# A PEER encoder layer on one core: packed rows, their waits, pinned TensorE work and smaller caps

## The chip, the core and the metric

The kernel runs on one core of a Trainium2 chip. The time is device time in microseconds (us) of one execution; several executions are timed and their median is given, and one more execution is recorded by the profiler. Engines by their names in the profile: PE is TensorE (PEld its weight loads), DVE is VectorE, ACT is ScalarE, POOL is GpSimd, SP is SyncE, which here only issues DMAs. Each engine, and each issuing queue, runs its instructions in order.

## The reference

One encoder layer for 256 tokens of width 2048: a mixer (grouped attention and a bidirectional mLSTM), cross-attention, and a PEER layer, each followed by a layer norm. The change touches the PEER layer only. There each token has 8 heads, and each head picks 16 of 16384 single-neuron experts by product keys; `u` and `v` hold one row of 2048 for each expert:

```python
experts = jnp.take_along_axis(cand_e..., best_pos, axis=-1)     # 128 experts per token
gates = jax.nn.softmax(best_s, axis=-1)
def block(args):
    xb, eb, gb = args
    a = jax.nn.gelu(jnp.einsum('ted,td->te', u[eb], xb), approximate=False) * gb
    return jnp.einsum('te,ted->td', a, v[eb])
```

## The kernel before

The PEER part computes the hidden values of *all* experts for all tokens, multiplies them by gates that are zero for what a token did not pick, and then brings only the experts that some token picked into a packed table, in whose order the rows of `v` are fetched.

U phase: the experts go in 32 quads of 512. `Ugen(q)` (L745) projects the 256 tokens on quad q in four chunks; each loads 1 MB of `u` into one of 5 `raw` buffers (`u_r`, L140, on SP), splits it in a high part (ScalarE, L103) and a low part (VectorE, L104), and runs 24 matmuls (L156, L157, L160). After the fourth chunk ScalarE applies Gelu (`gh`, L752). 11 quads (`LEAD`) run ahead while experts and gates are worked out; the gates go to DRAM (`gate_dram`, L812).

A phase: `Agen(q)` transposes `gh` of quad q on TensorE (L946, tile `ta`), multiplies by the gates (`G`, one load of 1 MB per two quads, L900; L949), writes the dense rows to DRAM (L959) and issues four indirect scatters on POOL (L962), each of 128 expert rows into `table`. Where a row goes is worked out for each pair g of quads in two steps: `route(g)` loads `G` and marks with masks M which expert serves both token tiles, only the first or only the second (kinds 0, 1, 2); `places(g, M)` counts them with two small matmuls (L914, L915; tile `pp`), scans, and leaves indices in `idx`. The table has room for `CAPS` tiles of 128 rows of each kind. An `Agen` gives way at three points: after each half of the transposes and after the scatters; that of quad 0 at seven more, between `route(0)` and `places(0)`.

V phase: `Vstage(n, lo, hi)` works on the table's tiles between two entries of `STAGES`, in two halves of 1024 columns. An entry such as `(16, (4, 2, 2))` says: once 16 scatters are out, 4, 2 and 2 tiles of the kinds are full. For one or two tiles it loads packed rows (`ar`, L1013, on SP), splits them (`ah`, `al`), gathers rows of `v` on POOL (L1024), splits these (`vh`, `vl`) and adds with three matmuls for each token tile and column block into PSUM (`o`, L1036): 24 matmuls for both halves of a tile of kind 0, 12 for one of kinds 1 and 2. From quad 14 (`VFROM`) on, U's sums lie in other PSUM banks and the `o` tiles have those of before.

The order in which these are traced is written out at the end: behind each chunk of U come `a_step` (three steps of `Agen` per chunk until the buffers of the first quads are given to `v`, then two) and `v_step` (some 3.6 us of V work per chunk, from quad 14 on; a stage starts 3 steps after its scatters were traced). The framework then places every instruction on its engine's queue by a simulated timeline, so it may run ahead of its traced order where its inputs are thought to be there sooner. After the loop a flag says whether the caps were overrun; if so, a branch does the V part densely.

The waits of the table loads are made by hand:

```python
for x in scat[covered[0]:]:
    tc.add_manual_dep(ins.ins, x.name, sync_data, reason="rows of the table")
covered[0] = len(scat)
```

`scat` holds all scatters traced so far, and each load waits for those that no load before it has waited for.

Of the kernel before, what the change touches and what calls it, by code (L numbers as in the profile page):

```python
# [18 lines left out]
P = 128  # L19
T = 256  # L20
# [9 lines left out]
LEAD = 11  # L30
# [5 lines left out]

CAPS = (53, 32, 32)
BASE = (0, CAPS[0], CAPS[0] + CAPS[1])  # L40
PLACES = sum(CAPS) * P
STAGES = ((16, (4, 2, 2)), (40, (13, 7, 7)), (72, (25, 14, 14)), (96, (34, 19, 19)), (112, (40, 23, 23)), (128, CAPS))


def body(tc, x, xT, memT, w_inA, w_inB, b_igate, b_fgate, att_q_norm, att_k_norm, ml_norm, w_out,
# [4 lines left out]
    V, S, G, PE = nc.vector, nc.scalar, nc.gpsimd, nc.tensor  # L50
# [37 lines left out]
    ident = cp.tile([P, P], F32, name="ident")  # L88
# [570 lines left out]
    table = dram.tile([PLACES, ROW], F32, name="table")  # L659
# [86 lines left out]
    ghs = {}  # L746
# [143 lines left out]
    nv = [0]  # L890
    Gt = {}
    run = [run0]
    scat = []
    covered = [0]
    sync_data = mybir.DependencyInfo(mybir.DependencyClass.Sync, mybir.DependencyReason.DATA)
# [14 lines left out]

    def places(g, M):
        pp = tp_tile(f"pp{g}")
        Mf = M.rearrange("p k i -> p (k i)")
        PE.matmul(pp[:, 0:24], before_m, Mf, start=True, stop=True)  # L914
        PE.matmul(pp[:, 24:48], ones_m, Mf, start=True, stop=True)  # L915
        inc = rtp.tile([P, 3, 8], F32, name=f"inc{g}", tag="inc")
        for k in range(3):
            V.tensor_tensor_scan(inc[:, k], pp[:, 24 + 8 * k:32 + 8 * k], zero8, run[0][:, k:k + 1], ALU.add, ALU.add)
        end = rtp.tile([P, 3], F32, name=f"end{g}", tag="end")
        V.tensor_copy(end, inc[:, :, 7])  # L920
        run[0] = end
        for n, (rows, _) in enumerate(STAGES):
            if rows == 8 * g + 8:
                V.tensor_copy(chk[:, n], inc[:, :, 7])
        V.tensor_tensor(inc.rearrange("p k i -> p (k i)"), inc.rearrange("p k i -> p (k i)"), pp[:, 24:48], ALU.subtract)
        V.tensor_tensor(inc.rearrange("p k i -> p (k i)"), inc.rearrange("p k i -> p (k i)"), pp[:, 0:24], ALU.add)
        V.tensor_tensor(inc, inc, M, ALU.mult)
        pf = rtp.tile([P, 8], F32, name=f"pf{g}", tag="pf")
        V.tensor_reduce(pf, inc.rearrange("p k i -> p i k"), AX.X, ALU.add)
        V.tensor_scalar(idx[:, g * 8:g * 8 + 8], pf, FAR, None, ALU.add)  # L930


    def Agen(q):
        if q == 0:
            M = route(0)
# [6 lines left out]
        for b in range(2):  # L942
            tp = tp_tile(f"ta{q}_{b}")
            for a in range(2):
                for t in range(NT):
                    PE.transpose(tp[:, a * T + t * P:a * T + (t + 1) * P],  # L946
                                 ghs[q][:, t, (2 * b + a) * P:(2 * b + a + 1) * P], ident)
            for a in range(2):
                V.tensor_tensor(r[:, 2 * b + a, :T].rearrange("p (c t) -> p c t", c=16),  # L949
                                tp[:, a * T:(a + 1) * T].rearrange("p (c t) -> p c t", c=16),  # L950
                                gg[:, :, (q % 2) * 4 + 2 * b + a, :], ALU.mult)
            if q % 2 == 1 and q + 1 < nq:
                if b == 0:
                    M = route((q + 1) // 2)
                else:
                    places((q + 1) // 2, M)
            yield
        ghs.pop(q)
        nc.sync.dma_start(dense[q], r)  # L959
# [29 lines left out]
    def Vstage(n, lo, hi):  # L989
# [9 lines left out]
        for half in range(2):  # L999
# [9 lines left out]
            for _, k, s0, w in order:  # L1009
# [1 line left out]
                ar = arp.tile([P, 2, ROW], F32, name=f"ar{nm}", tag="ar")[:, :w]  # L1011
                r0 = (BASE[k] + s0) * P
                ins = nc.sync.dma_start(ar, table[r0:r0 + w * P, :].rearrange("(p g) w -> p g w", p=P))  # L1013
                for x in scat[covered[0]:]:
                    tc.add_manual_dep(ins.ins, x.name, sync_data, reason="rows of the table")
                covered[0] = len(scat)
                tc.add_to_no_dep_group("table", ins.ins)
                c0, cw = ((0, T), (0, P), (P, P))[k]
                ah = ahp.tile([P, 2, T], F32R, name=f"ah{nm}", tag="ah")
# [211 lines left out]
```

## Time and profile before

| what | value |
|---|---|
| timed executions, median (3) | 2230.35 us (2224.93 to 2233.83) |
| profiled execution, whole | 2223.21 us |
| its span, first to last instruction | 2221.1 us |
| TensorE busy | 2120.2 us (95%) |
| VectorE, ScalarE, POOL busy | 1494.2, 1107.4, 452.7 us |
| matmuls of o (L1036) | 3 groups of 680 |
| scatters, gathers of v, table loads | 128, 234, 128 |

Times inside the execution are counted from the span's start. An engine's busy time counts its own instructions, not its waits; where an instruction waited, the profile names the idle time before it and the event that came last. The granted clock is a share of TensorE's full 2.4 GHz; it has two levels, 1.0 and 0.5, so a mean between them says for which part of a stretch the lower one held. The DMA share is the mean busy share of the core's 16 DMA engines.

### The profile page before, as it was taken

The page shows a single profiled execution, that of the slowest core. Times are in us where ns is not written, and L with a number is a line of the kernel's source. Part 1 is how long each engine was busy: PE and PEld are TensorE (multiplying, and loading weights), DVE is VectorE, ACT ScalarE, POOL GpSimd, SP SyncE. Part 2 cuts the span into 40 slices and gives each one's busy share as a digit, 9 for nine tenths or more (in the row PEclk, how much of TensorE's full clock was granted, in tenths as well). Part 3 has the DMA queues.
Part 4 walks back from the last instruction along what each step waited for, and adds up shares of the span by engine and source line. Part 5 has one row for each costly group of instructions (what it writes and reads, how often), then busy time and mean ns, then how long its engine had stood idle before and what let it go on. Part 6 is the DMA issues. An engine that isn't in the chain of part 4 may idle for free.

```text
span 2221.1 us, 28155 instructions
## 1 busy us (share of the span) xinstructions
PE 2120.2 (95%) x9794; PEld 1742.2 (78%) x9794; DVE 1494.2 (67%) x2678; ACT 1107.4 (50%) x1577; POOL 452.7 (20%) x402
## 2 busy tenths in 40 slices
PE   8899989999999899999997889999999999989996
PEld 6788868888888788888886668888877887868874
DVE  5765657664445679999785676676656656647776
ACT  4544635434443444579883244545454444536663
POOL 0000000000000000000002563443143434237661
PEclk9999989999999999999998989999999999989998
DMA  7543586565434345556668995987686778659994
GB/s 249 186 152 134 174 242 227 173 225 190 171 133 165 139 171 204 192 195 225 209 216 287 325 376 200 352 293 275 219 318 242 289 266 293 234 186 359 339 324 148
DMA packets 149479, 516.12 MB, mean 232 GB/s; under 512 B 14160, under 2 KB 59148, under 8 KB 113360
## 3 DMA queue, kind: packets, MB, share of 16 engines
q1 hardware_dynamic: 107504, 375.04, 48.7%
q0 software_dynamic: 39840, 137.19, 16.9%
q10 hardware_dynamic: 1984, 2.01, 0.3%
q8 instruction: 79, 1.29, 0.2%
q14 instruction: 72, 0.59, 0.1%
HBM read 457.72 MB, written 58.88 MB: 233 GB/s over the span
## 4 chain that ended last, share of the span: by engine, by line
PE 63%; issue 7%; DMA 5%; DVE 2%; POOL 2%; ACT 0%; POOLq 0%; DVEq 0%; SPq 0%; ACTq 0%
PE o L1036 17%; PE u_ps L156 8%; PE u_ps L160 8%; PE u_ps L157 8%; PE gp L808 3%; DMA table<-row,idx 2%; PE pq_ps L156 1%; PE wq_ps L160 1%; PE pq_ps L160 1%; PE pq_ps L157 1%; PE wq_ps L156 1%; PE wq_ps L157 1%; PE wv_ps L157 1%; PE wx_ps L156 1%; PE wx_ps L157 1%
## 5 line engine op out<-in xcount | busy, mean ns | idle before, releaser
L156 PE MATMUL u_ps<-u_h,x2T_h 128*128 128x512 f32 x1024 | 407.3, 398 | 4.3 <-ACT gh L752 4.3
L103 ACT CAST u_h<-u_r 128x1024 fp32r<-128x1024 f32 x256 | 268.7, 1051 | 275.0 <-PE u_ps L157 201.9
L157 PE MATMUL u_ps<-u_h,x2T_l 128*128 128x512 f32 x1024 | 404.4, 395 | 0.0
L104 DVE TENSOR_TENSOR u_l<-u_r,u_h 128x1024 fp32r<-128x1024 f32 x256 | 311.4, 1221 | 117.2 <-ACT u_h L103 111.3
L104 DVE TENSOR_TENSOR vl<-v,vh 128x1024 fp32r<-128x1024 f32 x234 | 285.4, 1224 | 138.9 <-ACT vh L103 130.1
L103 ACT CAST vh<-v 128x1024 fp32r<-128x1024 f32 x234 | 245.0, 1049 | 264.3 <-PE o L1036 103.6
L1024 POOL DMA_INDIRECT v<-in_peer_v_dram,ar x234 | 299.9, 1281 | 273.5 <-DMA ar<-table 114.1
L160 PE MATMUL u_ps<-u_l,x2T_h 128*128 128x512 f32 x1024 | 330.0, 397 | 0.6 <-DVE u_l L104 0.6
L962 POOL DMA_INDIRECT table<-row,idx x128 | 148.0, 1156 | 700.6 <-ACT u_h L103 433.5
L156 PEld LDWEIGHTS u_ps<-u_h,x2T_h 128*128 128x128 f32 x1024 | 193.1, 189 | 44.6 <-ACT gh L752 5.8
L157 PEld LDWEIGHTS u_ps<-u_h,x2T_l 128*128 128x128 f32 x1024 | 193.2, 189 | 38.1
L160 PEld LDWEIGHTS u_ps<-u_l,x2T_h 128*128 128x128 f32 x1024 | 190.0, 188 | 38.5 <-DVE u_l L104 1.0
L1036 PE MATMUL o<-vh,ah 128*128 128x512 f32 x680 | 208.6, 404 | 9.3 <-ACT vh L103 9.3
L1036 PE MATMUL o<-vl,ah 128*128 128x512 f32 x680 | 200.9, 399 | 5.2 <-DVE vl L104 5.2
L1036 PE MATMUL o<-vh,al 128*128 128x512 f32 x680 | 205.1, 400 | 0.0
L1036 PEld LDWEIGHTS o<-vh,ah 128*128 128x128 f32 x680 | 128.2, 191 | 39.5 <-ACT vh L103 11.0
L1036 PEld LDWEIGHTS o<-vl,ah 128*128 128x128 f32 x680 | 127.9, 190 | 37.7 <-DVE vl L104 7.6
L1036 PEld LDWEIGHTS o<-vh,al 128*128 128x128 f32 x680 | 129.8, 191 | 31.6
L156 PE MATMUL p_ps<-p_h,xT_h 128*128 128x512 f32 (+1 forms) x288 | 112.1, 391 | 8.0 <-ACT p_h L103 8.0
L104 DVE TENSOR_TENSOR p_l<-p_r,p_h 128x1024 fp32r<-128x1024 f32 (+2 forms) x74 | 83.6, 1137 | 50.0 <-ACT p_h L103 49.4
L103 ACT CAST p_h<-p_r 128x1024 fp32r<-128x1024 f32 (+2 forms) x74 | 71.9, 982 | 87.0 <-PE p_ps L157 70.1
L157 PE MATMUL p_ps<-p_h,xT_l 128*128 128x512 f32 (+1 forms) x288 | 110.9, 387 | 0.0
(383 smaller groups left out, 3555.7 us busy)
## 6 DMA issues: line engine op xcount, KB each, us to landing
u_r<-in_peer_uT_dram SPq DMA_DIRECT2D x128, 1024.0 KB, 6.5
p_r<-in_w_inA_dram SPq DMA_DIRECT2D x31, 1024.0 KB, 4.8
ar<-table SPq DMA_DIRECT2D x106, 258.0 KB, 4.9
dense<-row SPq DMA_DIRECT2D x32, 516.0 KB, 7.7
wo_r<-in_w_out_dram SPq DMA_DIRECT2D x16, 1024.0 KB, 4.9
wk_r<-in_xa_wk_dram SPq DMA_DIRECT2D x16, 1024.0 KB, 4.9
wv_r<-in_xa_wv_dram SPq DMA_DIRECT2D x16, 1024.0 KB, 4.8
wq_r<-in_xa_wq_dram SPq DMA_DIRECT2D x16, 1024.0 KB, 4.8
```

Source lines behind the costliest of these rows:

```text
L103: S.copy(hi, src)
L104: V.tensor_tensor(lo, src, hi.bitcast(F32), ALU.subtract)
L156: PE.matmul(ps[t][:, :width], op[0][:, k, s], hv[:, kk, :], start=st, stop=False)
L157: PE.matmul(ps[t][:, :width], op[1][:, k, s], hv[:, kk, :], start=False, stop=False)
L160: PE.matmul(ps[t][:, :width], op[0][:, k, s], lv[:, kk, :], start=False, stop=sp)
L808: PE.matmul(gp[:, t1 * P:(t1 + 1) * P], ohj, ohi, start=True, stop=True)
L962: ins = G.indirect_dma_start(out=table, out_offset=bass.IndirectOffsetOnAxis(ap=idx[:, i:i + 1], axis=0), in_=r[:, a, :], in_offset=None, ...
L1024: G.indirect_dma_start(out=v, out_offset=None, in_=v_rows, in_offset=bass.IndirectOffsetOnAxis(ap=ar[:, a, T + half:T + half + 1].bitcast( ...
L1036: PE.matmul(o[t][c], l_, r[:, c * 512:(c + 1) * 512], start=first[t] == (k, s0 + a) and i == 0, stop=last[t] == (k, s0 + a) and i == 2)
```

## The change

- A table load waits for the scatters of its own stage that no load waited for before (`scat[covered[0]:STAGES[n][0]]`), and the framework is told that the load has no other dependence on the group of the scatters.
- The first count matmul of `places`, and the first transpose of each half of quads 0 to 11, are pinned behind what was traced before them on TensorE (`keep_in_program_order`: the order of issue, no wait for the result).
- `route(g + 1)` is called in the second half of the even quad, `places(g + 1)` in the second half of the odd one; both were called in the odd quad, in the first and the second half.
- The caps go from 53, 32, 32 tiles to 52, 31, 31. The last stage, which ends at the caps, goes from 13, 9, 9 tiles to 12, 8, 8, and the zero fill of these tiles with it.

```diff
--- before.py
+++ after.py
@@ -36,7 +36,7 @@
 
 
 
-CAPS = (53, 32, 32)
+CAPS = (52, 31, 31)
 BASE = (0, CAPS[0], CAPS[0] + CAPS[1])
 PLACES = sum(CAPS) * P
 STAGES = ((16, (4, 2, 2)), (40, (13, 7, 7)), (72, (25, 14, 14)), (96, (34, 19, 19)), (112, (40, 23, 23)), (128, CAPS))
@@ -890,6 +890,7 @@
     nv = [0]
     Gt = {}
     run = [run0]
+    Ms = [None]
     scat = []
     covered = [0]
     sync_data = mybir.DependencyInfo(mybir.DependencyClass.Sync, mybir.DependencyReason.DATA)
@@ -911,7 +912,7 @@
     def places(g, M):
         pp = tp_tile(f"pp{g}")
         Mf = M.rearrange("p k i -> p (k i)")
-        PE.matmul(pp[:, 0:24], before_m, Mf, start=True, stop=True)
+        tc.keep_in_program_order(PE.matmul(pp[:, 0:24], before_m, Mf, start=True, stop=True))
         PE.matmul(pp[:, 24:48], ones_m, Mf, start=True, stop=True)
         inc = rtp.tile([P, 3, 8], F32, name=f"inc{g}", tag="inc")
         for k in range(3):
@@ -943,17 +944,19 @@
             tp = tp_tile(f"ta{q}_{b}")
             for a in range(2):
                 for t in range(NT):
-                    PE.transpose(tp[:, a * T + t * P:a * T + (t + 1) * P],
-                                 ghs[q][:, t, (2 * b + a) * P:(2 * b + a + 1) * P], ident)
+                    ins = PE.transpose(tp[:, a * T + t * P:a * T + (t + 1) * P],
+                                       ghs[q][:, t, (2 * b + a) * P:(2 * b + a + 1) * P], ident)
+                    if a == t == 0 and q <= LEAD:
+                        tc.keep_in_program_order(ins)
             for a in range(2):
                 V.tensor_tensor(r[:, 2 * b + a, :T].rearrange("p (c t) -> p c t", c=16),
                                 tp[:, a * T:(a + 1) * T].rearrange("p (c t) -> p c t", c=16),
                                 gg[:, :, (q % 2) * 4 + 2 * b + a, :], ALU.mult)
-            if q % 2 == 1 and q + 1 < nq:
-                if b == 0:
-                    M = route((q + 1) // 2)
+            if b == 1 and q + 2 < nq:
+                if q % 2 == 0:
+                    Ms[0] = route(q // 2 + 1)
                 else:
-                    places((q + 1) // 2, M)
+                    places(q // 2 + 1, Ms[0])
             yield
         ghs.pop(q)
         nc.sync.dma_start(dense[q], r)
@@ -1011,9 +1014,11 @@
                 ar = arp.tile([P, 2, ROW], F32, name=f"ar{nm}", tag="ar")[:, :w]
                 r0 = (BASE[k] + s0) * P
                 ins = nc.sync.dma_start(ar, table[r0:r0 + w * P, :].rearrange("(p g) w -> p g w", p=P))
-                for x in scat[covered[0]:]:
+                rows = scat[covered[0]:STAGES[n][0]]
+                covered[0] = STAGES[n][0]
+                tc.declare_no_dep(ins.ins, group="table", keep=rows, reason="other places")
+                for x in rows:
                     tc.add_manual_dep(ins.ins, x.name, sync_data, reason="rows of the table")
-                covered[0] = len(scat)
                 tc.add_to_no_dep_group("table", ins.ins)
                 c0, cw = ((0, T), (0, P), (P, P))[k]
                 ah = ahp.tile([P, 2, T], F32R, name=f"ah{nm}", tag="ah")
```

## Rows read from the trace of the kernel before

**Rows 1.** The page, first lines: span; each engine's busy time and share.

```profile
span 2221.1 us, 28155 instructions
...
PE 2120.2 (95%) x9794; PEld 1742.2 (78%) x9794; DVE 1494.2 (67%) x2678; ACT 1107.4 (50%) x1577; POOL 452.7 (20%) x402
```

**Rows 2.** Stretches: us, each engine's busy time, clock, DMA share, GB/s.

```profile
1175.00:1325.00 150.00, 120.09 (x556) 97.89 (x557) 97.58 (x208) 48.46 (x54) 77.83 (x70) 0.87 0.96 342
1325.00:1950.00 625.00, 618.31 (x2761) 501.53 (x2760) 397.91 (x545) 298.87 (x344) 224.26 (x179) 1.00 0.76 271
1950.00:2000.00 50.00, 40.66 (x156) 31.73 (x155) 24.66 (x31) 19.80 (x23) 22.16 (x20) 0.86 0.57 196
...
1187.00:1259.00 72.00, 71.58 (x343) 58.76 (x343) 57.12 (x119) 27.43 (x30) 35.00 (x30) 0.97 0.95 329
1259.00:1294.00 35.00, 17.22 (x77) 13.49 (x76) 17.80 (x64) 4.44 (x7) 22.35 (x23) 0.66 0.98 321
```

**Rows 3.** TensorE by time: start, us, line, operation, [idle before <-its end].

```profile
1186.71 0.20 PE L914 MATMUL pp<-M,before_m 128*128 128x24 bf16 x1 [13.06 <-DVE M L908]
...
1269.55 0.19 PE L914 MATMUL pp<-M,before_m 128*128 128x24 bf16 x1 [3.95 <-DVE row L949]
...
1277.60 1.94 PE L946 MATMUL ta<-ident,gh 128*128 128x128 f32 x8 [5.25 <-DVE idx L930]
...
1285.95 0.20 PE L914 MATMUL pp<-M,before_m 128*128 128x24 bf16 x1 [6.41 <-DVE M L908]
...
1974.36 1.22 PE L1036 MATMUL o<-vh,ah 128*128 128x512 f32 x2 [4.16 <-ACT vh L103]
...
1990.81 1.22 PE L1036 MATMUL o<-vh,ah 128*128 128x512 f32 x2 [5.18 <-ACT vh L103]
```

**Rows 4.** ScalarE in order of time, columns as in rows 3.

```profile
1186.22 1.99 ACT L103 CAST u_h<-u_r 128x1024 fp32r<-128x1024 f32 x2 [12.89 <-DMA u_r<-in_peer_uT_dram]
...
1257.51 1.09 ACT L752 ACTIVATE gh<-u_ps 128x512 f32<-128x512 f32 x2 [2.49 <-PE u_ps L160]
...
1281.66 0.62 ACT L103 CAST ah<-ar 128x512 fp32r<-128x512 f32 x1 [23.07 <-DMA ar<-table]
```

**Rows 5.** SP's queue in order of time: DMA issues, equal neighbours merged.

```profile
1178.76 0.33 SPq L900 DMA_DIRECT2D G<-gate_dram  x1
1179.18 1.55 SPq L140 DMA_DIRECT2D u_r<-in_peer_uT_dram  x3
...
1276.52 0.32 SPq L1013 DMA_DIRECT2D ar<-table  x1
...
1965.15 0.80 SPq L1013 DMA_DIRECT2D ar<-table  x2
...
1981.76 30.93 SPq L1013 DMA_DIRECT2D ar<-table  x13
```

**Rows 6.** POOL in order of time, columns as in rows 3.

```profile
1227.45 0.98 POOL L962 DMA_INDIRECT table<-row,idx  x1 [0.31 <-issue]
...
1267.96 0.98 POOL L962 DMA_INDIRECT table<-row,idx  x1 [0.31 <-issue]
...
1962.65 0.98 POOL L962 DMA_INDIRECT table<-row,idx  x1 [0.30 <-issue]
...
1978.58 0.98 POOL L962 DMA_INDIRECT table<-row,idx  x1 [0.30 <-issue]
```

**Rows 7.** Groups by line, 1960 to the end: busy us, mean ns | idle.

```profile
L1036 PE MATMUL o<-vh,ah 128*128 128x512 f32 x310 | 97.0, 406 | 9.3 <-ACT vh L103 9.3
```

**Rows 8.** One stretch of 25 us near the end, columns of rows 2.

```profile
2050.00:2075.00 25.00, 25.00 (x109) 20.12 (x108) 18.76 (x22) 16.09 (x20) 17.93 (x13) 1.00 0.94 324
```

**Rows 9.** What SP's queue waited for, 1325 to 1985: us, times, longest us.

```profile
SPq L140 <- DVE u_l L104: 218.2, 39, 10.8
SPq L1013 <- DMA table<-row,idx: 93.6, 23, 11.1
```

**Rows 10.** The page, DMA issues: count, KB each, median us to landing.

```profile
u_r<-in_peer_uT_dram SPq DMA_DIRECT2D x128, 1024.0 KB, 6.5
```

## The prediction

> **What bounds the kernel now.** I read the page's first part, then busy time by stretch, then the idle intervals of TensorE with what ended them, and last the queues that stood behind those. The profiled execution takes 2223.2 us, 2221.1 of it span [rows 1]; it lies 7 us under the median of 2230.35, so what I work out on it is moved up by 7 us at the end. TensorE is busy 2120 us of 2221 [rows 1]: the kernel is bound by its matmuls, and only two things shorten it, fewer matmuls or fewer holes between them. Up to about 1173 us nothing of the change runs but the zero fill of the table's tail, which gets smaller. Behind that, TensorE is 618 of 625 us busy in the long middle (1325 to 1950); the holes that the change can reach are in two places, 1175 to 1325 (30 us idle, clock 0.87) and 1950 to 2000 (9 us idle, clock 0.86) [rows 2].
>
> The first place has two parts. At 1186.7 TensorE comes out of a wait of 13.1 us for the mask M of the first count matmul, and between 1259 and 1294 it is idle 17.8 of 35 us, in waits of 4.0, 5.2 and 6.4 us and smaller ones, ended by VectorE [rows 2, 3]. What matters there is what TensorE did *not* have: new chunks of U. ScalarE, which casts them, stood 23.1 us on one cast, ah<-ar, for the first packed rows of the table [rows 4]. Those were issued at 1276.5 [rows 5]. The scatters show why: four per quad, the 16th starts at 1227.5 and the 36th at 1268.0 [rows 6]; stage 0 needs 16, but the load was traced when 34 steps of Agen had run (three per chunk for eight chunks of U, then two for five), that is quads 0 to 8, 36 scatters, and it waits for all of them. The 36th has landed some 8 us after its start, just ahead of 1276.5. ScalarE runs in order, so U14's casts stood behind this one.
>
> The second place is the same thing at the other end. From 1960 on there are 3 x 310 = 930 matmuls of o [rows 7], of which the last stage has 13 x 24 + 18 x 12 = 528; 402 belong to stages 3 and 4, whose rows were complete quads ago. Yet table loads go out at 1965.2 and 1981.8 [rows 5], 2.5 and 3.2 us behind the last scatters of quads 30 and 31 (1962.7 and 1978.6) [rows 6], and TensorE waits 4.2 and 5.2 us for vh of those rows [rows 3].
>
> **The caps.** A tile of kind 0 costs 3 x 2 x 2 matmuls per half, 24 in all, one of kinds 1 and 2 costs 12: before 53 x 24 + 64 x 12 = 2040, after 52 x 24 + 62 x 12 = 1992, 48 fewer, all in the last stage, where TensorE has no other work. In that stretch 109 matmuls go by in 25.00 us [rows 8], 0.229 us each: **-11.0 us**. With them go 6 gathers of v and 6 table loads, which lie beside the matmuls. Bounds: 48 x 0.2 and, if the transfers bound there, 6 of 234 gathers more, so -10 to -13. Less room could overflow: the reference's own expert choice, counted on its inputs, needs 6414, 3878 and 3733 rows of 6656, 3968 and 3968, so the fallback branch stays shut unless 90 rows change kind.
>
> **Own scatters only, first stage.** The 23.1 us stall of ScalarE loses its cause: 16 scatters are out by 1227.5 plus landing, 20 us before PSUM for o is free (the Gelu that ends U13 starts at 1257.5 [rows 4]). U14's first loads have then landed too. Recoverable are 17.8 us of idle time, plus the low clock: 0.66 over 35 us is 23.8 us at the lower level (1.2 of 2.4 GHz) [rows 2], of which between 6 us (all idle time in it) and 17.2 us (all busy time in it) was work at half speed, worth 3 to 8.6 us; I take 5. So 0 to 26, in all likelihood not all, because the DMA engines are at 0.98 in these 35 us [rows 2] and the new work needs gathers of v: I take two thirds of 23, **-15 us**. The Trainium skill (DMA: Bandwidth & Descriptors, Issuing engines are not separate DMA queues) says that transfers started by different engines run on the same 16 DMA engines and interleave. The share of 0.98 agrees that there was little room; by that rule alone the earlier loads would only displace others, and the gain here would be 0 instead of 15.
>
> **Own scatters only, end.** The waits of 4.2 and 5.2 us go, and the clock: 0.86 over 50 us is 14 us at the lower level, 2.3 to 7 us of loss; I take 5. In all 14.4, bounds 0 (the gathers still stand behind quad 31's scatters in POOL's order) and 16.5: **-12 us**. What is late next: stage 5 alone still needs scatter 128, landed at about 1982, and 402 matmuls x 0.23 = 92 us of stages 3 and 4 cover that. In between SP no longer stands on L1013 for scatters, 93.6 us in 23 waits between 1325 and 1985 [rows 9]; TensorE is busy there anyway, so I count nothing.
>
> **Pins.** The first count matmul now stands behind U11's chunks 0 to 2, and the first transpose of each half quad up to quad 11 behind the U chunks traced before it. The wait of 13.1 us stays, I think: U11's next chunks come from loads that SP issues at 1179.2, behind G's load at 1178.8, and ScalarE's cast of them starts at 1186.2 [rows 4, 5], half a us before M. Gain 0 to 15, I take 0. Behind the pinned matmul wait the index, the scatters on POOL and the table loads: two chunks of 24 x 0.229 = 5.5 us later, so scatter 16 at about 1240, still ahead of 1257. A loss is possible where a pinned instruction meets late data: TensorE is in order, and the nearest rows are the single waits of 4.0 and 6.4 us [rows 3].
>
> **Routes earlier.** route(g) moves from the odd quad's first half to the even quad's second half, with its load of G (1 MB, on SP), its reduction on VectorE and its slot among 5 raw buffers. G is then held three U quads instead of two, so on average half a slot more is missing for U's loads, which already wait for slots: 218.2 us in 39 waits of SP [rows 9]. A chunk's turn is some 10 us (18 quads of four chunks between 1257.5 [rows 4] and 1965), its load lands in 6.5 us [rows 10] and a cast takes 1 us [rows 4]; with 3 slots a load is still out two turns ahead, 20 us for some 9 of landing and splitting. Cover holds, cost 0; without it up to 6.5 us for each of 9 quads, 58 us. For pins and routes together I put **+3 us**, bounds -15 and +58.
>
> **Sum.** 2223 - 11 - 15 - 12 + 3 = 2188, against the median **2195 us**.
>
> **Rivals.**
> - *Everything is recovered*, the 13.1 us and its low clock (about 15 us) too, because the new order lets U's loads pass G's: 11 + 23 + 14 + 15 = 63, 2167 us. For it: the pin gives TensorE two chunks to do. Against: SP's order [rows 5] isn't pinned. 0.12.
> - *The DMA engines bound the first place*: they are at 0.96 over 150 us, where 0.76 follows [rows 2]. What isn't waited for in the table is waited for in u_r or v; only caps and half the end count: 11 + 6 = 17, 2213 us. 0.14. The rule of the Trainium skill named above would come out here.
> - *The scheduler's new order eats it*: it places instructions by simulated times, and every queue is laid anew; new holes of 4 to 6 us like those of [rows 3], six or seven of them, and 2223 to 2230 remains. 0.11.
> - *Slower: G's slot.* If SP stands on a U load for its slot so long that landing comes later than TensorE's need (from about 11 us of delay on), every second quad from U14 pays up to 6.5 us, and the table loads behind it on SP too: 2195 + 58 = 2253 us. Against: TensorE's 618 of 625 us [rows 2] say that U's loads come in time now. 0.08.
> - *The forecast*, 2180 to 2207: 0.55.
>
> **How the numbers follow.** A measurement of this kernel tells 0.5% (11 us) from no change. Faster by more (under 2219): forecast, everything, DMA: 0.81. Within 0.5%: 0.11. Slower: 0.08. The range leaves out half of "everything" below and the slow rival and a part of the new order above: 2166 to 2226.
>
> **What would show it.** Caps: 1992 matmuls of o instead of 2040, and a last stage of 480. Own scatters: the first load of ar leaves SP near 1240 to 1260, not behind the 36th scatter; ScalarE's cast of ah has no wait of 23 us; the stretch behind U13 has under 8 us of idle time at clock 1.0; table loads of stages 3 and 4 leave between 1935 and 1975 without waiting for L962. Pins: the wait that ends at 1186.7 ends on U's cast instead of M, with about the same length. Routes: u_r's waits on ScalarE stay near zero. I am wrong if TensorE's idle time between 1250 and 1330 stays over 15 us, or new idle time on u_ps appears after 1330.

## The result and the profile after

The changed kernel takes 2194.87 us in the median (2193.70 to 2196.38), the one before 2232.09 with the executions made beside it (2224.93 to 2234.92): 0.984 of it, with a 95% interval of 0.981 to 0.986. The forecast was 2195 us. The profiled execution is 2195.8 us, 27 us below the profiled one of before and 36 below the median: the profile of before happened to be the quickest execution of that kernel, and what another one loses more is found further down.

The page's first lines and the same stretches as in [rows 1] and [rows 2], of the changed kernel (us, then busy time of each engine, granted clock, DMA share, GB/s):

```profile
span 2193.9 us, 27979 instructions
...
PE 2107.1 (96%) x9746; PEld 1731.2 (79%) x9746; DVE 1483.8 (68%) x2666; ACT 1098.2 (50%) x1565; POOL 448.7 (20%) x396
```

```profile
1175.00:1325.00 150.00, 122.04 (x539) 96.15 (x540) 93.63 (x188) 49.01 (x56) 69.63 (x61) 0.91 0.89 323
1325.00:1950.00 625.00, 621.25 (x2784) 504.37 (x2783) 401.51 (x568) 297.68 (x344) 242.10 (x198) 1.00 0.81 284
1950.00:2000.00 50.00, 50.00 (x221) 40.67 (x220) 35.01 (x41) 30.18 (x37) 21.26 (x19) 1.00 0.68 218
...
1187.00:1259.00 72.00, 64.39 (x292) 51.44 (x292) 48.53 (x108) 22.05 (x26) 29.68 (x27) 0.93 0.82 287
1259.00:1294.00 35.00, 28.09 (x126) 21.21 (x124) 17.27 (x35) 11.59 (x13) 17.02 (x17) 0.99 0.98 383
```

TensorE's holes at the end are gone: 50.0 of 50.0 us busy at clock 1.00 from 1950 to 2000, where [rows 2] had 40.7 at 0.86. The first place has gained next to nothing in sum (122.0 of 150 us against 120.1), but the idle time has moved: the piece behind U13 has 28.1 of 35 us busy (17.2 before), the piece ahead of it 64.4 of 72 (71.6 before). TensorE by time, the longest holes, and ScalarE, columns as in rows 3 and 4:

```profile
1186.14 0.80 PE L156 MATMUL u_ps<-u_h,x2T_h 128*128 128x512 f32 x1 [13.47 <-ACT u_h L103]
...
1238.36 1.07 PE L947 MATMUL ta<-ident,gh 128*128 128x128 f32 x4 [4.86 <-DVE row L952]
...
1285.27 0.50 PE L156 MATMUL u_ps<-u_h,x2T_h 128*128 128x512 f32 x1 [1.65 <-ACT u_h L103]
...
1293.05 1.08 PE L947 MATMUL ta<-ident,gh 128*128 128x128 f32 x4 [2.58 <-DVE row L952]
```

```profile
1185.04 1.99 ACT L103 CAST u_h<-u_r 128x1024 fp32r<-128x1024 f32 x2 [12.70 <-DMA u_r<-in_peer_uT_dram]
...
1225.70 2.00 ACT L103 CAST u_h<-u_r 128x1024 fp32r<-128x1024 f32 x2 [10.09 <-DMA u_r<-in_peer_uT_dram]
...
1252.00 0.62 ACT L103 CAST ah<-ar 128x512 fp32r<-128x512 f32 x1 [1.37 <-DMA ar<-table]
```

The wait of 13 us stayed, and ends on U's cast instead of M. ScalarE waits 1.4 us for the first packed rows, 23.1 before; but 10.1 us for a load of U at 1225.7 (TensorE, which has other work, stands 0.8 us for that cast). SP's queue and POOL, columns as in rows 5 and 6:

```profile
1177.78 0.33 SPq L901 DMA_DIRECT2D G<-gate_dram  x1
1178.20 0.86 SPq L140 DMA_DIRECT2D u_r<-in_peer_uT_dram  x2
...
1219.23 0.32 SPq L962 DMA_DIRECT2D dense<-row  x1
1219.60 3.69 SPq L140 DMA_DIRECT2D u_r<-in_peer_uT_dram  x2
...
1248.51 1.93 SPq L1016 DMA_DIRECT2D ar<-table  x4
...
1944.39 27.29 SPq L1016 DMA_DIRECT2D ar<-table  x4
...
1975.28 31.46 SPq L1016 DMA_DIRECT2D ar<-table  x10
```

```profile
1207.40 1.34 POOL L965 DMA_INDIRECT table<-row,idx  x1 [448.49 <-PE ta L947]
...
1239.44 0.98 POOL L965 DMA_INDIRECT table<-row,idx  x1 [0.30 <-issue]
```

The first table loads leave at 1248.5, 28 us earlier than in [rows 5], behind the 16th scatter (1239.4) and not the 36th. The first scatter of all is 14 us later than before (1207.4; 1193.4 in the trace of before). And at 1219.2 stands a line to remember: a dense row, and 0.05 us behind its issue the loads of U for which ScalarE waits till 1225.7. At the end, the last table loads that [rows 5] had issued behind scatters at 1965 and 1982 begin at 1944. What answers to [rows 7], [rows 9] and [rows 10]:

```profile
L1041 PE MATMUL o<-vh,ah 128*128 128x512 f32 x294 | 89.2, 396 | 0.0
```

```profile
SPq L140 <- DVE u_l L104: 213.2, 34, 10.0
SPq L1016 <- DVE al L104: 104.2, 38, 10.0
```

```profile
u_r<-in_peer_uT_dram SPq DMA_DIRECT2D x128, 1024.0 KB, 6.0
```

From 1960 on 882 matmuls of o are left instead of 930, exactly the 48 of the caps; by then TensorE is no further ahead with V's work than before. SP's list for 1325 to 1985 has no line for L1016 (the table load's new line) behind a scatter; its longest wait for that load is now for the row buffers. U's waits for slots are as before (213 us), its landing too.

### The profile page after: what moved, and what is told of

It reads as the page before. It is cut to its first block, busy times and chain, and to the rows that moved or that the text cites. A ratio compares the mean times of both kernels' runs of the same rounds, so it can differ in the third digit from the quotient of the medians.

```text
span 2193.9 us, 27979 instructions
## 1 busy us (share of the span) xinstructions
PE 2107.1 (96%) x9746; PEld 1731.2 (79%) x9746; DVE 1483.8 (68%) x2666; ACT 1098.2 (50%) x1565; POOL 448.7 (20%) x396
## 3 DMA queue, kind: packets, MB, share of 16 engines
q0 software_dynamic: 38976, 134.04, 17.2%
## 4 chain that ended last, share of the span: by engine, by line
PE 50%; issue 22%; DMA 3%; DVE 2%; POOL 1%; ACT 0%; DVEq 0%; POOLq 0%; SPq 0%
PE o L1041 19%; PE u_ps L160 5%; PE u_ps L156 5%; PE u_ps L157 5%; DMA table<-row,idx 2%; PE wq_ps L160 1%; PE wq_ps L156 1%; PE wq_ps L157 1%; PE wv_ps L157 1%; PE wx_ps L157 1%; PE wx_ps L156 1%; PE wv_ps L160 1%; PE wv_ps L156 1%; PE wx_ps L160 1%; PE ta L947 1%
## 5 line engine op out<-in xcount | busy, mean ns | idle before, releaser
L1029 POOL DMA_INDIRECT v<-in_peer_v_dram,ar x228 | 288.7, 1266 | 376.0 <-DVE vl L104 169.9
L103 ACT CAST vh<-v 128x1024 fp32r<-128x1024 f32 x228 | 238.9, 1050 | 250.8 <-PE u_ps L157 105.9
L104 DVE TENSOR_TENSOR vl<-v,vh 128x1024 fp32r<-128x1024 f32 x228 | 277.7, 1223 | 128.1 <-ACT vh L103 113.6
L965 POOL DMA_INDIRECT table<-row,idx x128 | 155.1, 1212 | 577.9 <-PE ta L947 448.5
L1041 PE MATMUL o<-vl,ah 128*128 128x512 f32 x664 | 195.9, 399 | 4.4 <-DVE vl L104 4.4
L1041 PE MATMUL o<-vh,ah 128*128 128x512 f32 x664 | 199.1, 398 | 0.7 <-ACT vh L103 0.7
L1041 PE MATMUL o<-vh,al 128*128 128x512 f32 x664 | 198.1, 396 | 0.0
L1041 PEld LDWEIGHTS o<-vh,al 128*128 128x128 f32 x664 | 125.1, 188 | 29.7
L1041 PEld LDWEIGHTS o<-vh,ah 128*128 128x128 f32 x664 | 123.5, 189 | 29.2 <-ACT vh L103 1.9
```

The lines of the kernel that those rows point to most:

```text
L103: S.copy(hi, src)
L104: V.tensor_tensor(lo, src, hi.bitcast(F32), ALU.subtract)
L965: ins = G.indirect_dma_start(out=table, out_offset=bass.IndirectOffsetOnAxis(ap=idx[:, i:i + 1], axis=0), in_=r[:, a, :], in_offset=None, ...
L1029: G.indirect_dma_start(out=v, out_offset=None, in_=v_rows, in_offset=bass.IndirectOffsetOnAxis(ap=ar[:, a, T + half:T + half + 1].bitcast( ...
L1041: PE.matmul(o[t][c], l_, r[:, c * 512:(c + 1) * 512], start=first[t] == (k, s0 + a) and i == 0, stop=last[t] == (k, s0 + a) and i == 2)
```

## The experiments

To see what works where, each profile is cut at two marks: the end of the wait behind the gates (the row of about 13 us in TensorE's order of time), and the start of U's last matmul (the view of the tile u_ps). "Middle" is the time between the marks, "end" that from the second to the end of the span. The timed medians stand beside them.

| kernel | wait ends | U's last | span | middle | end | median us | to before, 95% |
|---|---|---|---|---|---|---|---|
| before | 1186.7 | 1966.1 | 2221.1 | 779.4 | 255.0 | 2230 to 2236 | |
| before_again | 1186.4 | 1974.9 | 2234.6 | 788.5 | 259.7 | 2236.8 (one) | |
| caps_only | 1183.8 | 1961.2 | 2203.8 | 777.4 | 242.6 | 2214.3 | 0.989 to 0.994 |
| own_only | 1185.8 | 1954.8 | 2197.4 | 769.0 | 242.6 | 2200.2 | 0.981 to 0.987 |
| after | 1186.1 | 1965.4 | 2193.9 | 779.3 | 228.5 | 2194.9 | 0.981 to 0.986 |
| no_pins | 1181.2 | 1950.2 | 2179.1 | 769.0 | 228.9 | 2177.3 | 0.971 to 0.975 |
| no_route | 1184.0 | 1956.1 | 2184.4 | 772.1 | 228.3 | 2187.9 | 0.977 to 0.980 |
| pin_count | 1184.1 | 1962.0 | 2188.4 | 777.9 | 226.4 | 2187.5 | 0.975 to 0.980 |
| np_nr | 1183.3 | 1953.3 | 2180.9 | 770.0 | 227.6 | 2182.3 | 0.973 to 0.978 |
| dense_pool | 1185.0 | 1952.4 | 2178.9 | 767.4 | 226.5 | 2181.8 | 0.973 to 0.979 |
| np_dense | 1183.3 | 1950.5 | 2176.9 | 767.2 | 226.4 | 2178.7 | 0.976 to 0.979 |
| no_own | 1184.1 | 2032.9 | 2273.7 | 848.8 | 240.8 | 2273.4 | 1.017 to 1.021 |

The medians of before differ by up to 6 us between the comparisons, so a few us are read from the stretches and the ratios together. Each stretch is from one profiled execution. The first mark itself lies between 1181.2 and 1186.7; no run explains these 5 us, and they are in the span too: of the 14.8 us between the profiles of the changed kernel and no_pins, 4.9 lie ahead of it. Two more kernels, in which the wait behind the gates itself is changed, have no first mark and stand at the end.

### Caps alone, own scatters alone

```diff
-CAPS = (53, 32, 32)
+CAPS = (52, 31, 31)
```

> The kernel before with the caps 52, 31, 31 and nothing else: 48 matmuls of o fewer at the end. Theory A (the parts of the change add up, and each works where its traces show it): 48 x 0.229 = 11 us less, 2219 to 2223 against 2232; the two waits for vh between 1970 and 1991 and the idle time between 1173 and 1325 stay as before. Theory B (a smaller change lays every queue anew, and that is worth more than the part): any time from 2205 to 2240, with idle time at other places than before.

The end falls from 255.0 to 242.6 us, 12.4 less, in the profile; the waits for vh near 1968 and 1986 (3.0 and 5.2 us) and those in the first place stay. That is theory A in the place and nearly in the size: TensorE's busy time in the end falls by 10.6 us (11.0 expected), its idle time by 1.9. The time itself was missed: the median is 22 us below that of before in the same comparison (13 to 26 by the interval), and 2214.3 lies under theory A's 2219 to 2223. The profiled execution is the quickest of this kernel, too; up to the end stretch it is 4.9 us shorter than before's as well, and what the timed ones gained beyond the 12.4 us is not shown. This kernel still has the old waits, and its spread (2206 to 2223 us) is as wide as that of before.

```diff
-                for x in scat[covered[0]:]:
+                rows = scat[covered[0]:STAGES[n][0]]
+                covered[0] = STAGES[n][0]
+                tc.declare_no_dep(ins.ins, group="table", keep=rows, reason="other places")
+                for x in rows:
                     tc.add_manual_dep(ins.ins, x.name, sync_data, reason="rows of the table")
-                covered[0] = len(scat)
```

> The kernel before with the table loads waiting for their own stage's scatters and nothing else; caps 53, 32, 32. Theory A (only the end gains: 9.3 us of idle time and about 5 us of low clock between 1950 and 2000, as the trace of the changed kernel has it): about 2217. Theory B (the prediction's: the first stage gains 15 us more): about 2202, with under 15 us of idle time of TensorE between 1187 and 1325 where before has 18. Theory C (the DMA engines bound the first place): as A, and idle time between 1187 and 1325 of 15 us or more, with a DMA share over 0.95.

Theory B. The end falls by 12.4 us (9.8 us of idle time, and 2.7 us of busy time for the same 934 matmuls, at a mean clock of 0.96 instead of 0.94), and the middle by 10.4. SP's first table loads, TensorE's longest hole behind them, and the stretch 1187 to 1325:

```profile
1235.25 3.51 SPq L1013 DMA_DIRECT2D ar<-table  x5
```

```profile
1280.66 1.94 PE L946 MATMUL ta<-ident,gh 128*128 128x128 f32 x8 [6.62 <-DVE row L949]
```

```profile
1187.00:1325.00 138.00, 127.95 (x593) 103.29 (x593) 98.99 (x200) 51.74 (x59) 73.24 (x64) 0.96 0.96 352
```

The loads leave at 1235, 41 us earlier than in [rows 5], and the idle time from 1187 to 1325 is 10.1 us (138 less 127.95). With a DMA share of 0.96 it was to be 15 or more by theory C, and before has 18.2 at 0.97: the DMA engines, as busy as before, did not stand in the way of this gain. What is left is for the most part one wait of 6.6 us on a transpose.

### The kernel before, once more

> The kernel before, unchanged, for a second profile: its timed executions lie between 2225 and 2241, the profiled one at 2223, the lowest of all. The changed kernel's lie within 3 us. Theory M (the executions differ in the places where a table load waits for scatters that it doesn't need): a profile of 2230 or more has its extra time as idle time of TensorE in 1259 to 1294 or 1950 to 2000, not in the first 1173 us. Theory N (they differ anywhere): the extra time is spread, or lies ahead of 1173 us, where the end of the gates moved by up to 5 us between the profiles so far.

This execution took 2236.8 us, 13.6 more than the profiled one of [rows 1]. The wait behind the gates ends at 1186.4 as there (1186.7); the middle is 9.1 us longer and the end 4.7. TensorE's holes, and ScalarE's wait for the first packed rows:

```profile
1281.27 1.94 PE L946 MATMUL ta<-ident,gh 128*128 128x128 f32 x8 [8.79 <-DVE idx L930]
...
1294.64 1.94 PE L946 MATMUL ta<-ident,gh 128*128 128x128 f32 x8 [6.87 <-DVE inc L926]
...
1999.42 1.22 PE L1036 MATMUL o<-vh,ah 128*128 128x512 f32 x2 [6.59 <-ACT vh L103]
```

```profile
1282.80 0.62 ACT L103 CAST ah<-ar 128x512 fp32r<-128x512 f32 x1 [21.47 <-DMA ar<-table]
```

In [rows 3] the longest holes of the first place were 5.2 and 6.4 us; here they are 8.8 and 6.9, and the idle time from 1187 to 1325 is 24.0 us against 18.2. So the middle bears theory M out: this kernel loses more or less time where a load waits for scatters that it doesn't need. The end does so only in part: its two waits for vh are 9.9 us in all (3.3 and 6.6) against 9.3, and 3.0 of its 4.7 us are one wait for vh at 2164.6, long after the last scatter (own_only has one like it, at 2130.4). Against this execution own_only's middle is 19.5 us shorter (788.5 - 769.0), against the first 10.4.

### The pins and the routes

```diff
-        tc.keep_in_program_order(PE.matmul(pp[:, 0:24], before_m, Mf, start=True, stop=True))
+        PE.matmul(pp[:, 0:24], before_m, Mf, start=True, stop=True)
...
-                    if a == t == 0 and q <= LEAD:
-                        tc.keep_in_program_order(ins)
```

> The changed kernel without its pins (count matmuls and first transposes free again). Theory A (the pins put the A phase some 14 us later, its dense writes stand ahead of U's loads on SP, and that took back what the first stage gained): idle time between 1187 and 1325 falls from 17.5 us to under 8, and the time to 2180 to 2187. Theory C (the DMA engines bound the first place, whatever the order): within 4 us of 2195, idle time as before. Theory D (the pins are needed): TensorE stands on a count matmul at 1187 for M again and on later ones, 2200 or more.

Theory A, though its time, 2180 to 2187, was too high, and the quickest version by the ratio: 2177.3 us, 17.5 less than the changed kernel. The middle falls from 779.3 to 769.0 us, just what own_only has; in the profiles the pins took back all that the early loads had gained there. The first scatter is at 1189.9 again:

```profile
1189.94 1.23 POOL L963 DMA_INDIRECT table<-row,idx  x1 [435.82 <-PE u_ps L157]
```

Idle time from 1187 to 1325 is 10.9 us (138 less 127.08), 16.8 in the changed kernel (the 17.5 of the expectation is 0.7 too high). It was expected under 8, and is not: one wait of 7.9 us on a transpose remains. The wait behind the gates ends on M again at 1181.2, after 13.2 us: theory D saw that rightly, and it costs nothing against the pinned kernel's 13.5 us on U's cast.

```diff
-                    if a == t == 0 and q <= LEAD:
-                        tc.keep_in_program_order(ins)
```

> The changed kernel with the count matmuls pinned and the transposes of quads 0 to 11 free. Both pins together cost 10.3 us between the end of the gates and the last matmul of U (779.3 against 769.0 us). Theory E (the count matmul's pin does it: the first scatter goes from 1193 to 1207 because the first count waits behind two chunks of U): as the changed kernel, some 779 us in that stretch and 2193 to 2197. Theory F (the transposes' pins do it: TensorE stands in order on transposes whose row buffers are still being written out, 4.9 us at 1238 and 2.6 us at 1293): as without pins, some 769 us and 2175 to 2182.

The middle is 777.9 us: theory E. In the profiles the count matmul's pin makes 8.9 of the 10.3 us, those of the transposes 1.4. The timed median (2187.5) lies between the two theories' ranges, 7 us under the changed kernel, so the transposes' pins may cost more in other executions than in the profiled one.

```diff
-            if b == 1 and q + 2 < nq:
-                if q % 2 == 0:
-                    Ms[0] = route(q // 2 + 1)
-                else:
-                    places(q // 2 + 1, Ms[0])
+            if q % 2 == 1 and q + 1 < nq:
+                if b == 0:
+                    Ms[0] = route((q + 1) // 2)
+                else:
+                    places((q + 1) // 2, Ms[0])
```

> The changed kernel with route(g + 1) and places(g + 1) both in the odd quad again. Prediction: the earlier route costs about 3 us by G's raw buffer, so 2192 here. Theory A (U's loads have room to spare, the move does nothing by itself): 2193 to 2197. Theory D (the earlier route covers the wait for M at the pinned count matmuls): here up to two waits of 4 to 6 us for M come back between 1230 and 1310, 2200 to 2207.

2187.9 us, below all that was expected, and a middle of 772.1: with the pins, the earlier routes cost 7 us. The next run takes back both.

> The changed kernel without pins and with route and places both in the odd quad: only the caps and the own-scatter waits are left. With the pins, taking back the routes gave 7 us. Theory G (G's raw buffer, held longer, costs by itself): 5 to 7 us less than without pins alone, 2170 to 2173. Theory H (the cost lies in the two together): equal to without pins, 2175 to 2181. Theory I (without pins the earlier route pays): 2182 or more. By the sum of the parts (caps 12 us at the end, own scatters 12 at the end and 10 before it) it is 2232 to 2236 less 35, about 2199, by the profiled run of before 2188.

A middle of 770.0 us (769.0 without pins alone) and 2182.3 us in the median (2177.3): without pins the earlier routes cost nothing, and perhaps give a few us. By the middle that is theory H; the time lies at the edge of theory I's range (2182 or more), and the two ratios overlap (0.971 to 0.975, 0.973 to 0.978), so I is not excluded. The middles of the four kernels with both the caps and the own-scatter waits: 770.0 us with neither pins nor earlier routes (np_nr), 772.1 with pins alone (no_route), 769.0 with earlier routes alone (no_pins), 779.3 with both. The cost lies in the two together. The sum of the parts, 2188 on the profile of before, was 5 us too high for the profiled execution (2182.7), 3 of them ahead of the first mark.

### The pins and what stands behind the dense rows

```diff
-        nc.sync.dma_start(dense[q], r)
+        G.dma_start(dense[q], r)
         for a in range(4):
```

> The changed kernel, pins and all, with the dense rows written out from POOL's queue, ahead of the scatters that wait for the same rows, instead of SP's: the same bytes, but U's loads don't stand behind a wait for rows any more (37 us of such waits on SP between 1187 and 1300). Theory A (the pins' cost comes from the dense writes that stand ahead of U's loads on SP): idle time between 1187 and 1325 from 17.5 to under 10 us, 2180 to 2188. Theory C (the DMA engines bound that stretch): within 4 us of 2195. Theory L (POOL needs longer for such a write than SP and holds up the gathers): 2200 or more.

Theory A. With pins and routes as changed, only the dense rows written from POOL, the middle falls from 779.3 to 767.4 us and the median to 2181.8. The first scatter is hardly earlier (1206.1), but U's loads that stood behind a dense row at 1219.6 now leave at 1213.2, and where the changed kernel issues no load of U between 1270 and 1295, dense_pool issues three from 1278.5 on. First dense_pool, then SP's queue in the changed kernel and its waits for dense rows from 1187 to 1300 (us, times, longest us):

```profile
1213.18 2.90 SPq L140 DMA_DIRECT2D u_r<-in_peer_uT_dram  x2
...
1278.51 17.17 SPq L140 DMA_DIRECT2D u_r<-in_peer_uT_dram  x3
```

```profile
1270.12 0.43 SPq L140 DMA_DIRECT2D u_r<-in_peer_uT_dram  x1
...
1293.60 0.32 SPq L962 DMA_DIRECT2D dense<-row  x1
1294.72 0.33 SPq L140 DMA_DIRECT2D u_r<-in_peer_uT_dram  x1
...
SPq L962 <- DVE row L952: 37.0, 7, 13.7
```

The longest of these waits, 13.7 us, is the one that ends at 1293.6.

The stretch 1187 to 1325 of four kernels, in this order: the changed one, dense_pool, np_dense and no_pins (us, busy times of TensorE, its loads, VectorE, ScalarE, POOL; clock, DMA share, GB/s):

```profile
1187.00:1325.00 138.00, 121.18 (x538) 95.39 (x538) 89.94 (x184) 47.05 (x55) 69.63 (x61) 0.94 0.89 323
```

```profile
1187.00:1325.00 138.00, 129.31 (x600) 103.19 (x599) 99.94 (x206) 50.95 (x59) 82.11 (x76) 0.97 0.93 339
```

```profile
1187.00:1325.00 138.00, 133.63 (x620) 107.52 (x620) 99.84 (x204) 52.89 (x60) 86.47 (x79) 0.97 0.95 354
```

```profile
1187.00:1325.00 138.00, 127.08 (x604) 103.32 (x603) 97.65 (x199) 51.31 (x59) 79.92 (x67) 0.98 0.95 348
```

The changed kernel keeps the DMA engines least busy (0.89) *and* TensorE (121.2 us): so its loads were late because SP held them, and not because the engines were full. np_dense moves 354 GB/s at a share of 0.95, while between 1259 and 1294 a share of 0.98 went with 321 GB/s [rows 2].

That the 12 us hang on the dense rows' place on SP is shown by this run, as far as one move can show it (with every edit the framework lays all queues anew; that the same move gives nothing without pins, in the next run, speaks for the queue). Which load behind them counts is not shown. TensorE's idle time in this stretch is 16.8 us in the changed kernel and 8.7 in dense_pool: 8.0 against 5.2 in waits of transposes for the row, 3.5 against none in waits for U's casts. And G's loads and the first table loads leave SP earlier as well (1247.2 against 1252.3, 1243.9 against 1248.5). Nor is it the length of SP's waits: np_nr's SP stands 35.7 us on dense rows between 1187 and 1300, nearly the changed kernel's 37.0, with a middle of 770.0. So what counts must be which loads stand behind, and when; pins and routes decide that together.

Without pins, and with dense rows from POOL:

> The changed kernel without pins and with the dense rows written from POOL's queue. With the pins the move gave back 12 us (779.3 to 767.4 us between the end of the gates and U's last matmul); without pins that stretch is 769.0 already. If both cure the same stall (U's loads behind a dense write on SP): 2174 to 2180, the stretch within 4 us of 768. If they are two things: some 10 us less, 2165 to 2170.

2178.7 us and a middle of 767.2, as for one stall and not two.

### The own-scatter wait taken back from the changed kernel

```diff
-                rows = scat[covered[0]:STAGES[n][0]]
-                covered[0] = STAGES[n][0]
-                tc.declare_no_dep(ins.ins, group="table", keep=rows, reason="other places")
-                for x in rows:
+                for x in scat[covered[0]:]:
                     tc.add_manual_dep(ins.ins, x.name, sync_data, reason="rows of the table")
+                covered[0] = len(scat)
```

> The changed kernel with the table loads waiting for all scatters traced so far again; pins, routes and caps as changed. By the parts: the stretch after the last matmul of U goes from 228.5 to about 241 us, and the one before it from 779 to at most 790, so 2207 to 2220. If the own-scatter waits are worth only the idle time at the end: 2207 to 2210. If the pins alone already take the load's early start away (the first load then has fewer scatters ahead of it): the stretch before stays at 779.

2273.4 us, far outside everything expected, and slower than the kernel before (by 1.7 to 2.1%). The end is 12.3 us longer, as the parts say, but the middle is 69.5 us longer than in the changed kernel. TensorE's four holes and ScalarE's waits:

```profile
1291.47 2.07 PE L1039 MATMUL o<-vh,ah 128*128 128x512 f32 x4 [18.04 <-ACT vh L103]
...
1323.02 1.22 PE L1039 MATMUL o<-vh,ah 128*128 128x512 f32 x2 [17.08 <-ACT vh L103]
...
1356.46 2.07 PE L1039 MATMUL o<-vh,ah 128*128 128x512 f32 x4 [13.02 <-ACT vh L103]
...
1395.23 2.07 PE L1039 MATMUL o<-vh,ah 128*128 128x512 f32 x4 [11.30 <-ACT vh L103]
```

```profile
1283.29 0.62 ACT L103 CAST ah<-ar 128x512 fp32r<-128x512 f32 x1 [15.91 <-DMA ar<-table]
...
1316.82 0.41 ACT L103 CAST ah<-ar 128x256 fp32r<-128x256 f32 x1 [20.48 <-DMA ar<-table]
...
1383.59 0.62 ACT L103 CAST ah<-ar 128x512 fp32r<-128x512 f32 x1 [22.28 <-DMA ar<-table]
```

The four holes are 59.4 us, and they look alike: ScalarE stands on the cast of packed rows (15.9, 20.5, 22.3 us; 5.8 ahead of the third hole), behind it U's casts; the loads of these rows wait for scatters of later quads; and those scatters' transposes are pinned behind U chunks that need ScalarE's casts. One round of it: TensorE goes on at 1291.5 with V's matmuls and a chunk of U and reaches the next transposes at 1305.3, the scatter follows at 1306.6, the table load at 1314.2, ScalarE's cast at 1316.8, TensorE's next matmul of o at 1323.0. So, by this trace, pins and the old wait hold each other up; no run with the old wait has the pins without the routes. The parts don't simply add: the own-scatter waits are worth 36 us by themselves and 78 beside pins and routes, and pins with routes cost 9 us in the middle with the new waits (779.3 - 770.0) but 71 with the old (848.8 - 777.4).

### The wait behind the gates

Gate writes from ScalarE and the first load of G from POOL, pins off:

```diff
-                nc.sync.dma_start(gd[:, :, tch, :], ...)
+                S.dma_start(gd[:, :, tch, :], ...)
...
-        nc.sync.dma_start(gr_, gd[:, g].rearrange("p c w -> p (c w)"))
+        (G if g == 0 else nc.sync).dma_start(gr_, gd[:, g].rearrange("p c w -> p (c w)"))
```

> The changed kernel without pins, with the writes of the gates issued by ScalarE (which has just filled them) instead of SP, and the first load of G by POOL. It tests the reading of the wait of 13 us at the end of the gates: SP stands on the gate writes, and U's loads stand behind it. Theory A (that is the cause): U11's chunks are loaded before, the wait falls to under 3 us and the low clock with it, 10 to 15 us less than without pins, 2162 to 2168. Theory J (what is missing there is a free raw buffer or TensorE's work for M): the wait stays, 2175 to 2180. Theory K (ScalarE is held up by issuing): 2180 to 2190.

2186.2 us, slower than without pins alone, and neither theory A's time nor J's. It is K's time, but ScalarE's issuing does not show as the cause: its last two gate writes take 0.5 us each, and the next kernel, which writes the gates in the same way, takes 2175.9 us. TensorE's holes, and SP:

```profile
1171.83 0.50 PE L156 MATMUL u_ps<-u_h,x2T_h 128*128 128x512 f32 x1 [1.81 <-ACT u_h L103]
...
1190.16 1.22 PE L160 MATMUL u_ps<-u_l,x2T_h 128*128 128x512 f32 x2 [8.62 <-DVE u_l L104]
```

```profile
1175.65 0.33 SPq L901 DMA_DIRECT2D G<-gate_dram  x1
1176.07 1.23 SPq L140 DMA_DIRECT2D u_r<-in_peer_uT_dram  x2
```

The hole of 13.2 us became 1.8 and 8.6: U11's chunk 1 was there in time, so SP's order had made that wait, but now the *second* load of G stood on SP for the gates, and U's next loads 0.4 us behind it. The rest was lost further on: the idle time from 1187 to 1325 is 18.1 us, 10.9 without pins alone; why is not shown. With the first three loads of G and the dense rows on POOL too:

> As the kernel without pins and with dense rows from POOL, and besides the gate writes issued by ScalarE and the first three loads of G by POOL, so that nothing that waits for the gates stands ahead of U's loads on SP; the run with only the first of them moved had the wait of 13 us split in 1.8 and 8.6, because the second G load stood on SP. Theory A: U11's chunks 1 and 2 run while the gates travel, the idle time between 1165 and 1200 falls to under 4 us, 10 to 14 us less than with dense rows from POOL alone, 2162 to 2169. Theory J (the idle time moves to the next place, because the A phase bounds the start of V): 2172 to 2180, with new idle time between 1200 and 1300.

```profile
1172.66 0.50 PE L156 MATMUL u_ps<-u_h,x2T_h 128*128 128x512 f32 x1 [1.81 <-ACT u_h L103]
...
1186.61 1.22 PE L160 MATMUL u_ps<-u_l,x2T_h 128*128 128x512 f32 x2 [4.25 <-DVE u_l L104]
...
1247.16 1.23 PE L160 MATMUL u_ps<-u_l,x2T_h 128*128 128x512 f32 x2 [3.47 <-DVE u_l L104]
```

The holes between 1165 and 1200 are 1.8 and 4.3 us, 6.1 in all and 7 less than without the move, but the median is 2175.9 us, not told apart from np_dense's 2178.7 or the 2177.3 without pins; new holes such as the one of 3.5 us at 1247 have taken the rest. Theory J. The ratios to before of these three (0.974 to 0.978, 0.976 to 0.979, 0.971 to 0.975) order them otherwise than the medians do, with no_pins ahead, so they are not ranked here. All three beat the changed kernel by some 16 to 19 us.

## Why the prediction was right, and where it was not

- **What bounds it.** Right: of the 27.2 us between the two profiled spans, 13.1 are TensorE's busy time (48 matmuls and less low clock) and 14.1 its idle time. The two places were the right ones, but the gain came in the second: the end is 26.5 us shorter, the middle 0.1.
- **Caps, -11.** 12.4 us in the end stretch of caps_only, within the bounds of 10 to 13; its timed executions gained more, 13 to 26 us, and why is open. The fallback branch stayed shut: the trace has 1992 matmuls of o.
- **Own scatters, end, -12.** 12.4 us against the profile of [rows 1], with 2.7 us for the low clock where 5 were put (the upper bound, by its own terms 9.3 and 7, is 16.3 and not 16.5). The late table loads began at 1944 instead of waiting for the scatters of quads 30 and 31, and stage 5 waited for nothing that the 92 us of cover didn't hide.
- **Own scatters, first stage, -15.** 10.4 us against the profile of [rows 1], 19.5 against the second profile of before: the size lay between. The mechanism, ScalarE on ah<-ar and U's casts behind it, is borne out by own_only and, from the other side, by no_own. That the DMA engines were at 0.98 was no good reason to take a third off: own_only gained at 0.96, and what it did not gain is for the most part one wait on a transpose. The Trainium skill's rule (DMA: Bandwidth & Descriptors, Issuing engines are not separate DMA queues), that all transfers share the same 16 engines, gave a gain of 0 as the prediction read it; at a share of 0.96 own_only gained the 10.4 us all the same. The section's second half, that issuing from several engines saves only the time to initiate, does not hold here where a waiting write stands ahead: moving the dense rows to POOL gave back 12 us.
- **Pins and routes, +3.** The step that failed in size: 9.3 us in the middle by np_nr, 10.3 by own_only. The prediction followed the pinned count matmul to the index, the scatters on POOL and the table loads, found scatter 16 at "about 1240, still ahead of 1257" (it was 1239.4), and concluded that nothing was lost. It left out what else stands behind the same rows: the dense write on SP, which issues in order, and the loads behind *that*. Taking the dense writes off SP gave back 11.9 us; that it was U's loads that counted is argued, not shown. The routes' slot among the raw buffers, which it feared, did not show by itself: without pins they cost nothing, and only with them 7 us. It put one term for both and had no step in which the two meet.
- **The sum.** On the profiled execution it was 2188, and the profiled execution of the changed kernel is 2195.8: 8 us more. The middle gained 0.1 us instead of 12 (4.6 too few from the own scatters, 7.3 too many for pins and routes), the end 26.5 instead of 23. The shift of 7 us to the median then brought it to 2195. But that shift belongs to the kernel before: the changed kernel's median lies 0.9 us *under* its profiled execution, and its executions within 3 us of each other. The second profile of before shows why in part: two thirds of what it loses more lie in the middle, at a place that the change mends. Two errors of some 8 us cancelled, and that the median came out at 2194.9 is luck.
- **The rivals.** "Everything is recovered" failed on the wait behind the gates, as argued. The DMA-bound rival is contradicted by own_only, and by dense_pool, which issues the same bytes in another order. The new order did eat something: the middle's gain, through pins and routes, but not the end's. The slower one did not occur; a slow outcome of 78 us did lie nearby, not in G's slot but in pins and routes without the new waits.

## What to carry to other kernels

When an instruction is pinned or moved, follow every queue on which something waits for its result, the unimportant writes too: a write that only a fallback reads can hold up the loads behind it on the same queue. A wait written as "all so far" ties a load to whatever happens to be traced ahead of it; let it name what it reads, or an engine in order further down (here ScalarE) passes the wait on to unrelated work. And before a sum is made on one profile, look at a second one: a place that varies from execution to execution can be worth more than one profile says.

## What the runs showed of the hardware

The DMA engines' busy share alone did not tell what they moved: 0.98 went with 321 GB/s in [rows 2] and with 383 in the changed kernel's same stretch, and 0.95 with 354 over 138 us in np_dense. In the profile of before each of the two holes near the end (4.2 and 5.2 us) was followed by the lower clock: the mean is 0.66 from 1970 to 1980 and from 1990 to 2000, and 1.00 in the ten us before, between and behind. In own_only, without these holes, it is 1.00 from 1950 to 2020.
